# Raw-residual quarter sums for the feed-forward input, and a PSUM tile of its own for the second product's sum

## The chip, the cores and the metric

One core of a Trainium2 chip runs the whole program. The metric is the device time of one execution in microseconds, median of the runs. TensorE (PE) multiplies, VectorE (DVE) and ScalarE (ACT) do the elementwise work, GpSimd (POOL) issues the accumulating DMAs, SyncE (SP) all others.

## The reference

One step of a 1-layer encoder on 512 prompt and 32 sample tokens (544 columns here). Before the part that is changed stand attention, a recurrent branch and cross-attention; then:

```
merged = gates[:, :, 0] * ya + gates[:, :, 1] * yb + gates[:, :, 2] * yc
x = x + merged @ lp["w_out"]
h2 = rms_norm(x, lp["norm_ffn"])
g_ff, u_ff = jnp.split(h2 @ lp["w_ffn_in"], 2, axis=-1)
x = x + (jax.nn.silu(g_ff) * u_ff) @ lp["w_ffn_out"]
```

`rms_norm` multiplies each token by one factor, 1/sqrt(mean(x*x) + 1e-6), and each of the 1024 features by its gain. `w_ffn_in` is 1024 x 5632 (2816 gate and 2816 up columns), `w_ffn_out` 2816 x 1024. A final rms_norm follows.

## The kernel before

Activations lie transposed: 128 partitions x 8 feature blocks x 544 tokens. Every fp32 operand is split into a high part (`wh`, `bh`, `ah`, `hh`, made by ACT) and a low part (`wl`, `bl`, `al`, `hl`, made by DVE as the difference, `LO`), and a product takes three matmuls: hi x hi, lo x hi of the activations, hi x lo. A plain `gemm` tile of the input (8 feature blocks, two halves of 272 tokens) is 48 matmuls.

A planner, `Flow`, sets the order of all engines: generators (`take`, `get`, `yield`) are resumed by estimated times, and the instructions are recorded as they come. The hardware follows that order per engine and waits only on semaphores, which are set per tile.

The output projection (`c_o`, 8 tiles of 48 matmuls) adds to the residual `x2` in `out_evac` and gathers the squares in `sqa`; `row_norm` makes from them the factor `rb` (a few 1-column matmuls, a root of small DVE operations, a broadcast by matmuls with `ident`).

The feed-forward part has 11 pairs of input chunks (256 gate and 256 up columns), in four parts of 3, 3, 3 and 2 pairs; the order of stages is input 0 and 1, output 0, input 2, output 1, input 3, output 2, output 3. An input chunk is done in one of two ways.

- Plain (`ffn_plain`): the first pair, from `xgh`, `xgl` (the residual times the gain, made in `out_evac`); `rb` is multiplied in at the evacuation (`ff_gate`, `ff_up`). Four tiles, 192 matmuls.
- Fast (`seven`): all other 20 chunks. A chunk is a 2 x 2 block product in seven products of 12 matmuls each, 84. They are called A11, A12, A22, P1 to P4; the activations' quarter sums (forms B11, B2, U1, U2, four feature-block pairs i each) come from `ff_forms`, those of the weights from POOL's accumulating DMAs and two DVE sums. `ff_forms` waits for `rb`, then for each i multiplies two blocks of `x2` by gain and `rb`, makes sums on DVE and splits them.

Order of the products on PE: A11 of chunk c, then A22 and P4 of chunk c-1, then A12, P2, P1, P3 of chunk c. A11, P2, P3 and A22 add up in `a`, which is read between them: ACT copies it after A11 (`c11`), P2 (`c12`) and P3 (`u3`). P1 and P4 go to `b` in a side tile. A12 goes to `c_`, the second half of the acc tile whose first half is `a`; DVE adds `c_` to the copy. PSUM holds two acc tiles (two banks each) and four side tiles.

Weights come through two `raw` slots: SP loads, POOL accumulates, and `split_ffn` makes hi and lo blocks of 512, in eight places per kind, which are free again when a product is done. The gate chunk's four quarters go through Silu (`fast_gate`), the up chunk's are multiplied to them (`fast_up`) and split into the activations of the output matmuls (`acts`, in `bh`/`bl` for even parts, `ah`/`al` for odd ones).

Of the kernel before, what the change touches and what calls it, by code (L numbers as in the profile page):

```python
# [10 lines left out]
F32R = mybir.dt.float32r  # L11
# [194 lines left out]
def hybrid_step(ctx: ExitStack, tc, io):  # L206
# [26 lines left out]
    for k_, n_ in NB.items():  # L233
        fl.bufs(k_, n_)

# [142 lines left out]
    FF_PLAIN = c_fi[0][0]  # L378
    FF_FAST = {c for part in c_fi for pair in part for c in pair} - set(FF_PLAIN)

# [65 lines left out]

    def split_ffn():

        for tag, w_ in (("wh", "hb"), ("wl", "lb")):
            for _ in range(NB[tag]):  # L450
                yield from fl.take(tag)
                w = slot_tile(wpool, [P, 8, P], F32R, tag).rearrange("p a b -> p (a b)")
                add_blocks(w_, [w[:, :512], w[:, 512:]])
# [3 lines left out]
        for i in order:  # L457
            nk = chunks[i][1]
            yield from fl.get(("raw", i, 0))
            if late is not None and i not in FF_FAST:  # L460
                yield from late
                late = None
            if i not in FF_FAST:
                for j in range(2):
                    if i in FF_PLAIN:
                        r = raws[i].rearrange("p a b -> p (a b)").rearrange("p (j e i c) -> p j e i c", j=2, e=2, i=4)
                        for e in range(2):
                            yield from split((i, j, e), r[:, j, e])
                        ks = [((i, j, k % 2), k // 2) for k in range(nk)]
                    else:  # L470
                        for e in range(0, nk, 4):
                            yield from split((i, j, e), raws[i][:, e:min(e + 4, nk), j * P:(j + 1) * P])
                        ks = [((i, j, k // 4 * 4), k % 4) for k in range(nk)]
                    wts[i, j] = tuple([blocks[b][a][:, q] for b, q in ks] for a in range(2))
                    names = sorted({b for b, _ in ks})
                    frees[i, j] = names
                    fl.set(("wh", i, j), max(fl.ev["bh", b] for b in names))
                    fl.set(("wl", i, j), max(fl.ev["bl", b] for b in names))
                fl.give("raw", max(fl.ev["bl", b] for b in names))
                continue  # L480
# [25 lines left out]
    def split_weights():  # L506
        for i, (src, nk) in enumerate(chunks):
            if i == FF_PLAIN[0]:
                yield from split_ffn()
                return  # L510
# [1110 lines left out]
    mh = ml = xgh = xgl = x2 = None  # L1621
# [19 lines left out]
    def out_evac(fp, n):  # L1641
        def go(acc):
# [21 lines left out]
    def ff_forms():  # L1664

        bt, blt, ht, hlt, mt = S["bh"], S["bl"], S["xhh"], S["xhl"], S["xm"]
        half = 4 * T
        two = lambda ap: ap.rearrange("p (i t) -> p i t", i=4)
        B11 = (two(bt[:, 6 * T:]), two(blt[:, 6 * T:]))
        B2 = (two(ht[:, :half]), two(hlt[:, :half]))  # L1670
        U1 = (two(ht[:, half:]), two(hlt[:, half:]))
        U2 = (two(mt[:, :half]), two(mt[:, half:]))
# [4 lines left out]
        yield from fl.take("ft", "ft", "ft")  # L1677
        scratch = [fl.pick("ft") for _ in range(3)] + [S["sq"][1]]
        yield from fl.get("rb")
        for i in range(4):  # L1680
            y0, y1, u1, u2 = scratch
            for q, y in enumerate((y0, y1)):
                t = VX(y, x2[:, 2 * i + q], vcol("norm_ffn", 2 * i + q), S["rb"], OP.mult, OP.mult)
            yield t
            A(B11[0][:, i], y0[:, lo])
            A(B2[0][:, i], y1)
            VT(u1[:, lo], y0[:, lo], y0[:, hi], OP.subtract)
            VX(u1[:, hi], u1[:, lo], -1.0, y1[:, hi], OP.mult, OP.subtract)
            VT(u2[:, lo], y1[:, hi], y0[:, hi], OP.subtract)
            t = VX(u2[:, hi], u1[:, hi], -1.0, y1[:, lo], OP.mult, OP.subtract)  # L1690
            fl.set(("xf", "B11", i), LO(B11[1][:, i], y0[:, lo], B11[0][:, i]))
            fl.set(("xf", "B2", i), LO(B2[1][:, i], y1, B2[0][:, i]))
            yield t
            for g, ev, u in ((U1, "U1", u1), (U2, "U2", u2)):
                yield A(g[0][:, i], u)
                t = LO(g[1][:, i], u, g[0][:, i])
                fl.set(("xf", ev, i), t)
        for y in scratch[:3]:
            fl.drop("ft", y, t)

    def seven(run):
# [20 lines left out]
        for c, evac in run + [(None, None)]:  # L1722
            if c is not None:
                yield from fl.take("acc")
                acc = slot_tile(accp, [P, 2, 512], F32, "acc")
                a, c_ = acc[:, 0, :HT], acc[:, 1, :HT]
                S["b", c] = None
                fl.spawn(evac(c, a, c_))
                yield from product(a, c, "A11", True, False)
            if prev is not None:  # L1730
# [4 lines left out]
            if c is None:  # L1735
                return
# [394 lines left out]
```

## Time and profile before

| | us |
|---|---|
| median of 3 runs | 1247.83 (1246.43 to 1248.45) |
| the profiled execution | 1245.97 |
| its span in the trace | 1243.9 |
| PE busy | 1197.2 (96%) |
| DVE busy | 772.8 (62%) |
| ACT busy | 537.0 (43%) |

Line numbers are those of the kernel; most instructions come from helpers (L325 all matmuls, L252 all ACT operations, L265 and L274 DVE operations), so a place is told by the tiles' names. Idle time of an engine stands in brackets with what ended it. The granted clock is TensorE's, 1.00 for the full rate.

### The profile page before, as it was taken

Reading aid. Unit: us, or ns where it says so; the run is one execution under the profiler, and the core shown is the slowest. Engines: PE = TensorE matmul, PEld = TensorE weight load, DVE = VectorE, ACT = ScalarE, POOL = GpSimd, SP = SyncE. Lnnn points to the kernel's source line nnn. Section 1 sums busy time; section 2 is a strip of 40 time slices with the busy share of each in tenths; the row PEclk is TensorE's granted clock in tenths of the full one; section 3 lists DMA queues with packets and bytes.
Section 4 is the critical chain, followed back from the end, with each engine's and each line's share of the span. In section 5 each row is a group of like instructions: output and inputs, shape, how many; then the busy total and the mean of one; then the engine's idle time right before and its main releaser. Section 6 shows DMA issues by size and latency. Waiting matters only on the chain.

```text
span 1243.9 us, 22824 instructions
## 1 busy us (share of the span) xinstructions
PE 1197.2 (96%) x9380; PEld 1180.2 (95%) x9380; DVE 772.8 (62%) x1594; ACT 537.0 (43%) x1013; POOL 63.5 (5%) x128
## 2 busy tenths in 40 slices
PE   8999999999999999999999999995999999998996
PEld 8999999999999999999999999995998999998996
DVE  6886878776258777545354334478676647736545
ACT  6635454444254666432233223354555435524422
POOL 0002000000001101000000000010111011011001
PEclk8999999999999999999999999997999999999998
DMA  7673342322132221423331322242555546454312
GB/s 261 236 261 110 136 134 96 111 82 85 68 111 77 97 91 68 154 79 108 119 119 68 148 95 91 79 116 63 128 153 136 152 116 146 123 143 119 119 52 72
DMA packets 51817, 146.95 MB, mean 118 GB/s; under 512 B 5848, under 2 KB 17496, under 8 KB 43648
## 3 DMA queue, kind: packets, MB, share of 16 engines
q1 hardware_dynamic: 45952, 135.01, 32.5%
q0 software_dynamic: 5760, 10.49, 5.4%
q8 instruction: 73, 1.20, 0.4%
q14 instruction: 32, 0.26, 0.1%
HBM read 134.54 MB, written 13.68 MB: 119 GB/s over the span
## 4 chain that ended last, share of the span: by engine, by line
PE 91%; DVE 6%; ACT 1%; issue 1%; DMA 1%; SPq 0%; DVEq 0%; ACTq 0%
PE acc L325 76%; PE side L325 13%; PE side L332 2%; DVE wl L265 1%; DMA raw<-in_w_mem_kv 1%; DVE t L265 1%; ACT wh L252 0%; DVE al L265 0%; DVE fq L265 0%; DVE x L274 0%; DVE hl L265 0%; DVE raw L265 0%; DVE fq L274 0%; DVE rst L265 0%; DVE bl L265 0%
## 5 line engine op out<-in xcount | busy, mean ns | idle before, releaser
L252 ACT ACTIVATE wh<-raw 128x1024 fp32r<-128x1024 f32 (+2 forms) x251 | 199.2, 801 | 259.7 <-PE acc L325 194.8
L265 DVE TENSOR_TENSOR wl<-raw,wh 128x512 fp32r<-128x512 f32 (+1 forms) x252 | 225.6, 905 | 125.7 <-PE acc L325 75.9
L325 PE MATMUL acc<-hh,wh 128*128 128x272 f32 x1268 | 274.0, 292 | 10.5 <-DVE fq L265 5.4
L325 PE MATMUL acc<-hl,wh 128*128 128x272 f32 x1268 | 270.8, 290 | 0.0
L325 PEld LDWEIGHTS acc<-hh,wh 128*128 128x128 f32 x1268 | 203.0, 189 | 14.3 <-DVE fq L265 6.3
L325 PEld LDWEIGHTS acc<-hl,wh 128*128 128x128 f32 x1268 | 202.6, 188 | 0.1
L325 PE MATMUL acc<-hh,wl 128*128 128x272 f32 x1268 | 180.9, 289 | 0.0
L325 PEld LDWEIGHTS acc<-hh,wl 128*128 128x128 f32 x1268 | 166.9, 188 | 0.1
L325 PE MATMUL acc<-bh,wh 128*128 128x272 f32 x464 | 100.3, 289 | 9.7 <-ACT bh L252 9.7
L325 PE MATMUL acc<-bl,wh 128*128 128x272 f32 x464 | 100.2, 290 | 2.4 <-DVE bl L265 2.4
L325 PE MATMUL acc<-ah,wh 128*128 128x272 f32 (+2 forms) x440 | 93.0, 289 | 0.0
L325 PE MATMUL acc<-al,wh 128*128 128x272 f32 (+2 forms) x440 | 92.9, 290 | 0.0
L325 PEld LDWEIGHTS acc<-bh,wh 128*128 128x128 f32 x464 | 74.9, 189 | 10.2 <-ACT bh L252 10.2
L265 DVE TENSOR_TENSOR x<-acc,x 128x544 f32<-128x544 f32 (+2 forms) x43 | 29.4, 685 | 88.9 <-PE acc L325 88.9
L325 PEld LDWEIGHTS acc<-bl,wh 128*128 128x128 f32 x464 | 74.9, 188 | 3.0 <-DVE bl L265 3.0
L325 PEld LDWEIGHTS acc<-ah,wh 128*128 128x128 f32 x440 | 70.0, 189 | 0.0
L325 PEld LDWEIGHTS acc<-al,wh 128*128 128x128 f32 x440 | 70.0, 189 | 0.0
L325 PE MATMUL acc<-bh,wl 128*128 128x272 f32 x464 | 67.8, 290 | 0.0
L325 PE MATMUL acc<-ah,wl 128*128 128x272 f32 (+2 forms) x440 | 62.4, 291 | 0.0
L325 PEld LDWEIGHTS acc<-bh,wl 128*128 128x128 f32 x464 | 61.8, 189 | 0.0
L325 PEld LDWEIGHTS acc<-ah,wl 128*128 128x128 f32 x440 | 58.6, 192 | 0.0
L401 POOL DMA_DIRECT2D raw<-in_w_ffn_in x20 | 17.4, 872 | 599.3 <-PE side L325 318.1
(317 smaller groups left out, 2030.9 us busy)
## 6 DMA issues: line engine op xcount, KB each, us to landing
raw<-in_w_in SPq DMA_DIRECT2D x24, 1024.0 KB, 4.9
raw<-in_w_gate SPq DMA_DIRECT2D x12, 1024.0 KB, 4.9
raw<-in_w_ffn_in SPq DMA_DIRECT2D x20, 512.0 KB, 4.5
raw<-in_w_ffn_in SPq DMA_DIRECT2D x40, 256.0 KB, 4.9
raw<-in_w_ffn_out SPq DMA_DIRECT2D x12, 768.0 KB, 4.3
raw<-in_w_mem_kv SPq DMA_DIRECT2D x7, 1024.0 KB, 5.5
fb<-in_w_ffn_in SPq DMA_DIRECT2D x20, 256.0 KB, 5.0
raw<-in_w_ffn_in POOLq DMA_DIRECT2D x20, 256.0 KB, 4.3
```

The costliest lines, as they stand in the source:

```text
L252: nc.scalar.activation(out, in_, func, scale=scale, bias=bias, accum_out=accum_out)
L265: nc.vector.tensor_tensor(out, a, b, o)
L325: nc.tensor.matmul(out, lhsT=lhsT, rhs=rhs, start=start, stop=stop, skip_group_check=shared)
L332: nc.tensor.transpose(out, in_, ident[:n, :n])
L401: nc.gpsimd.dma_start(b[:, 1536:], d[:, 1536:], accum_op=OP.add)
```

## The change

All 22 input chunks take the fast way; `ffn_plain`, `ff_gate`, `ff_up` and `xgh`, `xgl` are gone. `ff_forms(i)` is spawned once per i before the projection and starts when the two residual blocks it needs are there. It leaves `rb` out: ACT multiplies by the gain alone. `rb` comes later: on the gate's quarters ahead of Silu, and for the up side not at all in parts 0 to 2. There the sum in `x2` is kept divided by `rb` (`unnormalise`, a reciprocal and eight multiplications on DVE) and multiplied by `rb` after part 2's output; in part 3 the products are multiplied by `rb` themselves.

`c_` gets a side tile. The first output tile of a stage is put between the last chunk's P3 and its A22 (`between`), output tiles are issued one by one, and `split_ffn` fills its places and splits the late weights accordingly. The places of `ah`/`al` and `bh`/`bl` are swapped. The core of the diff:

```diff
-    FF_PLAIN = c_fi[0][0]
-    FF_FAST = {c for part in c_fi for pair in part for c in pair} - set(FF_PLAIN)
+    FF_FAST = {c for part in c_fi for pair in part for c in pair}
...
     def out_evac(fp, n):
...
-            yield A(xgh[:, n], x2[:, n], scale=vcol("norm_ffn", n))
-            t = VX(xgl[:, n], x2[:, n], vcol("norm_ffn", n), f(xgh[:, n]), OP.mult, OP.subtract)
-            fl.set(("xg", n), t)
+            fl.set(("x2", n), t)
             yield from square_sum(S["sq"][0], n)
...
+    def ff_forms(i):
+
+        B11, B2, U1, U2 = S["forms"]
+        lo, hi = slice(0, HT), slice(HT, T)
+        yield from fl.get(("x2", 2 * i), ("x2", 2 * i + 1))
+        yield from fl.take("ft", "ft", "ft", "sqb")
+        y0, y1, u1 = ys = [fl.pick("ft") for _ in range(3)]
+        u2 = S["sq"][1]
+        for q, y in enumerate((y0, y1)):
+            t = A(y, x2[:, 2 * i + q], scale=vcol("norm_ffn", 2 * i + q))
+        yield t
+        A(B11[0][:, i], y0[:, lo])
+        A(B2[0][:, i], y1)
+        VT(u1[:, lo], y0[:, lo], y0[:, hi], OP.subtract)
+        VX(u1[:, hi], u1[:, lo], -1.0, y1[:, hi], OP.mult, OP.subtract)
+        VT(u2[:, lo], y1[:, hi], y0[:, hi], OP.subtract)
+        t = VX(u2[:, hi], u1[:, hi], -1.0, y1[:, lo], OP.mult, OP.subtract)
+        yield t - 800
+        t = LO(B11[1][:, i], y0[:, lo], B11[0][:, i])
...
+    def unnormalise():
+
+        yield from fl.get("rb", *[("xf", "U2", i) for i in range(4)])
+        yield from fl.take("sqb")
+        ir = S["sq"][1]
+        yield VR(ir, S["rb"])
+        for k in range(KD):
+            t = VT(x2[:, k], x2[:, k], ir, OP.mult)
+            fl.set(("x2'", k), t)
+            yield t + 2000
...
     def seven(run, between=None):
...
-                a, c_ = acc[:, 0, :HT], acc[:, 1, :HT]
+                a = acc[:, 0, :HT]
...
+            elif between is not None:
+                yield from between
             if prev is not None:
                 yield from fl.get(("u3", prev[0]))
                 yield from product(prev[1], prev[0], "A22", False, True)
...
+            yield from fl.take("side")
+            S["c", c] = c_ = side_tile()[:, :HT]
             yield from product(c_, c, "A12", True, True)
...
     def fast_gate(i, n):
...
-                A(g[:, cs], src, AF.Silu, scale=-1.0 if j else 1.0)
+                if j:
+                    yield from fl.get("rb")
+                    VT(g[:, cs], src, S["rb"][:, cs], OP.mult)
...
+            fl.set(("fg", i, n, 1), A(g[1], g[1], AF.Silu, scale=-1.0))
+            yield VT(g[0], g[0], S["rb"], OP.mult)
+            fl.set(("fg", i, n), A(g[0], g[0], AF.Silu))
...
     def fast_up(i, n):
...
+                if i == NPART - 1:
+                    t = VT(u[j], u[j], S["rb"], OP.mult)
...
     def fo_evac(fp, i, n):
...
+            if i == NPART - 2:
+                yield t
+                VT(x2[:, n], x2[:, n], S["rb"], OP.mult)
...
+        for i in range(4):
+            fl.spawn(ff_forms(i))
+        fl.spawn(unnormalise())
...
-        fl.spawn(ff_forms())
-        yield from ffn_in(0, 1)
-        yield from ffn_out(fp, 0)
-        yield from ffn_in(2)
-        yield from ffn_out(fp, 1)
-        yield from ffn_in(3)
-        yield from ffn_out(fp, 2)
-        yield from ffn_out(fp, 3)
+        acts_order = [((0, 1), 0), ((2,), 1), ((3,), 2)]
+        for parts, q in acts_order:
+            yield from ffn_in(*parts, between=ffn_out(fp, q, 0, 1) if q < 3 else None)
+            yield from ffn_out(fp, q, 1)
+        yield from ffn_out(fp, NPART - 1)
```

The instructions' order shows three places. In these rows `DVE_49`, `Activation_49` and `PE_49` are the counters of DVE, ACT and PE that an instruction waits on, `DMASW` those of POOL's DMAs.

PE from the end of A12 into P2 of a fast chunk, before:

```order
L325 MATMUL acc<-hl,wh 128x272
L325 MATMUL acc<-hh,wl 128x272 x4
L325 MATMUL acc<-hh,wh 128x272
L325 MATMUL acc<-hl,wh 128x272
L325 MATMUL acc<-hh,wh 128x272 [waits DVE_49]
L325 MATMUL acc<-hl,wh 128x272
```

The same place of the changed kernel:

```order
L327 MATMUL side<-hl,wh 128x272
L327 MATMUL side<-hh,wl 128x272 x4
L327 MATMUL acc<-hh,wh 128x272 [waits Activation_49]
L327 MATMUL acc<-hl,wh 128x272
L327 MATMUL acc<-hh,wh 128x272
```

A12 writes a side tile now, and the wait on DVE ahead of P2's third matmul is gone; P2's first one waits for ACT's copy of `a` instead.

PE behind the projection, before (plain tiles from `ah`, `al`, with the norm's matmuls among them):

```order
L325 MATMUL acc<-ah,wh 128x272 x2
L325 MATMUL acc<-al,wh 128x272 x2
L325 MATMUL side<-ones_d,sqa 128x1 [waits DVE_49]
L325 MATMUL side<-ones_d,sqa 128x1 x4
L325 MATMUL acc<-ah,wh 128x272 x2
L325 MATMUL acc<-al,wh 128x272 x2
L325 MATMUL acc<-ah,wh 128x272 [waits Activation_49]
```

The changed kernel there; `ah`, `al` hold the form B11 now, and the rows are A11 of the first chunk:

```order
L327 MATMUL acc<-ah,wh 128x272 [waits Activation_49]
L327 MATMUL acc<-al,wh 128x272
L327 MATMUL side<-ones_d,sqa 128x1 [waits DVE_49]
L327 MATMUL side<-ones_d,sqa 128x1 x4
L327 MATMUL side<-ident,rsy_9384 128x128 [waits DVE_49]
L327 MATMUL side<-ident,rsy_9384 128x128 x3
L327 MATMUL side<-ident,rsy_9384 128x32
L327 MATMUL acc<-ah,wh 128x272 [waits Activation_49]
L327 MATMUL acc<-al,wh 128x272 [waits DVE_49]
L327 MATMUL acc<-ah,wl 128x272 x4
L327 MATMUL side<-hh,wh 128x272
```

Between the norm's two groups of matmuls stood plain tiles; now nothing stands there, and A11's last form comes behind the second group.

DVE behind the root, before (`fq` and `sqb` are the forms' scratch tiles, `rb` the factor):

```order
L281 COPY rb<-side 128x32 [waits PE_49]
L265 TENSOR_TENSOR wl<-raw,wh 128x512 [waits Activation_49]
L274 SCALAR_TENSOR_TENSOR fq<-x_8133,vec,rb 128x544 [waits DVE_49,Activation_49]
L274 SCALAR_TENSOR_TENSOR fq<-x_8133,vec,rb 128x544
L265 TENSOR_TENSOR t_9433<-acc,rb 128x544
L265 TENSOR_TENSOR fq<-fq 128x272 [waits DVE_49]
L274 SCALAR_TENSOR_TENSOR fq<-fq 128x272 [waits DVE_49]
L265 TENSOR_TENSOR sqb<-fq 128x272
```

The changed kernel, some rows behind the root:

```order
L267 TENSOR_TENSOR m<-sqb,m 128x544 [waits Activation_49]
L267 TENSOR_TENSOR wl<-raw,wh 128x512 [waits PE_49,Activation_49]
L267 TENSOR_TENSOR raw<-raw 128x512 [waits DMASW2_49]
L267 TENSOR_TENSOR fq<-side,fq 128x272 [waits PE_49,Activation_49]
L288 RECIPROCAL sqb<-rb 128x544 [waits DVE_49]
L267 TENSOR_TENSOR wl<-raw,wh 128x512 [waits Activation_49]
L267 TENSOR_TENSOR wl<-raw,wh 128x512 [waits PE_49,Activation_49]
L267 TENSOR_TENSOR wl<-fb,wh 128x512 [waits DMASW3_49,PE_49,Activation_49]
L267 TENSOR_TENSOR fq<-side,fq 128x272 [waits Activation_49]
L267 TENSOR_TENSOR x_8133<-x_8133,sqb 128x544 [waits DVE_49]
```

The forms' operations have left this place; the last form's last low part (`m`) is the first row, and the reciprocal and the first multiplication of `x2` by it stand among the first two chunks' work.

## Rows read from the trace of the kernel before

**Rows 1.** The page, part 1: busy us (share of the span) xinstructions.

```profile
PE 1197.2 (96%) x9380; PEld 1180.2 (95%) x9380; DVE 772.8 (62%) x1594; ACT 537.0 (43%) x1013; POOL 63.5 (5%) x128
```

**Rows 2.** Windows: length; busy PE, PEld, DVE, ACT, POOL; granted clock, DMA share, GB/s.

```profile
814.22:859.19 44.97, 31.92 (x226) 30.56 (x225) 40.13 (x81) 22.34 (x39) 4.70 (x6) 0.83 0.43 112
859.19:1167.17 307.98, 290.52 (x2247) 283.79 (x2247) 188.18 (x330) 140.50 (x292) 30.54 (x35) 1.00 0.51 132
...
850.00:858.00 8.00, 1.88 (x4) 0.96 (x4) 7.96 (x17) 3.99 (x7) 0.00 (x0) 0.50 0.51 157
858.00:861.00 3.00, 3.00 (x14) 3.00 (x15) 2.61 (x5) 1.18 (x2) 1.74 (x2) 0.53 0.41 63
```

**Rows 3.** PE timeline, the start of the feed-forward: start, us, instruction [idle before <-releaser].

```profile
818.33 1.28 PE L325 MATMUL side<-ones_d,sqa 128*128 128x1 f32 x10 [0.93 <-DVE sqa L265]
...
850.00 0.60 PE L325 MATMUL acc<-bh,wh 128*128 128x272 f32 x1 [6.01 <-ACT bh L252]
```

**Rows 4.** DVE timeline, behind the projection and in the forms.

```profile
814.42 0.72 DVE L265 TENSOR_TENSOR x<-acc,x 128x544 f32<-128x544 f32 x1 [3.06 <-PE acc L325]
...
819.64 0.16 DVE L269 TENSOR_SCALAR rs<-side 128x5 f32<-128x5 f32 x1 [0.16 <-PE side L325]
...
821.64 0.17 DVE L274 SCALAR_TENSOR_TENSOR rsy<-rst,rsy 128x5 f32<-128x5 f32 x1
...
845.78 0.71 DVE L265 TENSOR_TENSOR bl<-t,bh 128x544 fp32r<-128x544 f32 x1
846.42 0.68 DVE L265 TENSOR_TENSOR wl<-fb,wh 128x512 fp32r<-128x512 f32 x1
847.02 0.68 DVE L265 TENSOR_TENSOR wl<-raw,wh 128x512 fp32r<-128x512 f32 x1
...
849.65 0.44 DVE L265 TENSOR_TENSOR sqb<-fq 128x272 f32<-128x272 f32 x1
850.00 0.44 DVE L274 SCALAR_TENSOR_TENSOR sqb<-fq 128x272 f32<-128x272 f32 x1
```

**Rows 5.** ACT timeline, a weight split in the same stretch.

```profile
842.57 0.61 ACT L252 ACTIVATE wh<-fb 128x512 fp32r<-128x512 f32 x1
```

**Rows 6.** PE's waits, whole kernel: for whom: us in total, times, longest.

```profile
PE acc L325 <- DVE fq L265: 6.5, 10, 1.0
PE acc L325 <- DVE t L265: 5.4, 10, 0.6
...
PE acc L325 <- ACT fq L252: 2.9, 4, 1.3
```

**Rows 7.** The chain that ended last: P2 of two neighbouring chunks; output 0.

```profile
874.20 1.52 PE acc L325 x10
...
885.51 1.52 PE acc L325 x10
...
975.52 36.23 PE acc L325 x288
```

**Rows 8.** PE timeline: weight split, start of a run, end of a run.

```profile
948.04 0.39 PE L325 MATMUL acc<-bh,ah 128*128 128x272 f32 x1 [1.00 <-ACT ah L252]
...
1014.78 0.40 PE L325 MATMUL acc<-hh,ah 128*128 128x272 f32 x1 [1.28 <-ACT fq L252]
...
1079.41 1.27 PE L325 MATMUL acc<-m,ah 128*128 128x272 f32 x8 [0.49 <-ACT t L252]
```

**Rows 9.** DVE groups by form, whole kernel: reciprocals; busy us, mean ns.

```profile
L286 DVE RECIPROCAL cc<-sm 128x1 f32<-128x1 f32 x32 | 4.9, 154 | 1.9 <-ACT e L252 1.8
...
L286 DVE RECIPROCAL r<-sm 128x8 f32<-128x8 f32 x4 | 0.8, 197 | 0.0
...
L286 DVE RECIPROCAL sp_d<-sp_d 128x8 f32<-128x8 f32 x1 | 0.2, 202 | 0.0
```

**Rows 10.** POOL timeline: first and last of seven accumulations in the first run.

```profile
877.72 0.86 POOL L401 DMA_DIRECT2D raw<-in_w_ffn_in  x1 [17.84 <-DMA raw<-in_w_ffn_in]
...
957.80 0.86 POOL L401 DMA_DIRECT2D raw<-in_w_ffn_in  x1 [12.33 <-DVE al L265]
```

More of the change, by code (lines that the diff above doesn't have):

```diff
@@ L445, in add_blocks, with to_blocks, split_plain @@
         fl.ring(tag, aps)
-    def split_ffn():
[L449 to L453, printed above, removed]
+    def to_blocks(tag, ring):
+        yield from fl.take(tag)
+        w = slot_tile(wpool, [P, 8, P], F32R, tag).rearrange("p a b -> p (a b)")
+        add_blocks(ring, [w[:, :512], w[:, 512:]])
+    def split_plain(i, j):
+        nk = chunks[i][1]
+        for e in range(0, nk, 4):
+            yield from split((i, j, e), raws[i][:, e:min(e + 4, nk), j * P:(j + 1) * P])
+        ks = [((i, j, k // 4 * 4), k % 4) for k in range(nk)]
+        wts[i, j] = tuple([blocks[b][a][:, q] for b, q in ks] for a in range(2))
+        frees[i, j] = names = sorted({b for b, _ in ks})
+        fl.set(("wh", i, j), max(fl.ev["bh", b] for b in names))
+        fl.set(("wl", i, j), max(fl.ev["bl", b] for b in names))
+    def split_ffn():
+        for _ in range(NB["wh"]):
+            fl.spawn(to_blocks("wh", "hb"))
+            fl.spawn(to_blocks("wl", "lb"))
         order = [c for kind, q in FF_ORDER for c in
@@ L457, in split_ffn @@
         for i in order:
-            nk = chunks[i][1]
             yield from fl.get(("raw", i, 0))
-            if late is not None and i not in FF_FAST:
-                yield from late
-                late = None
             if i not in FF_FAST:
                 for j in range(2):
[L465 to L479, printed above, removed]
+                    yield from split_plain(i, j)
+                    if late is not None:
+                        yield from late
+                        late = None
+                fl.give("raw", fl.ev["wl", i, 1])
                 continue
@@ L1704, in product, with seven @@
+    def unnormalise():
[7 more added lines that the diff above has]
+            yield t + 2000
+    def seven(run, between=None):
         def product(dst, c, form, first, last):
@@ L1755, in quarters @@
         yield from fl.get(("done", c, "A12"))
-        t = VT(t0[:, lo], c_, t0[:, lo], OP.add)
+        t = VT(t0[:, lo], S["c", c], t0[:, lo], OP.add)
+        fl.give("side", t)
         yield t
-        each(t0, 0, lo, t0[:, lo])
+        yield from each(t0, 0, lo, t0[:, lo])
         yield from fl.get(("done", c, "P2"))
@@ L1778, in quarters @@
         yield t
-        each(t0, 0, hi, t0[:, hi])
+        yield from each(t0, 0, hi, t0[:, hi])
         return t0, t1
@@ L1860, in ffn_in @@
             acts[i] = [S[n][:, :6 * T].rearrange("p (k t) -> p k t", k=6) for n in x]
[L1861 to L1865 removed]
+        yield from seven(run, between)
     def fo_evac(fp, i, n):
         def go(acc):
+            yield from fl.get(("x2'", n))
             t = VT(b2(x2[:, n]), acc[:, :, :HT], b2(x2[:, n]), OP.add)
```

136 lines of the change are left out of this document (45 added, 91 removed).

## The prediction

> **What bounds the kernel now.** I read the page's busy shares first, then the windows, then PE's rows in the feed-forward part, then the orders. PE is busy 96% of the span [rows 1], so only fewer matmuls or fewer PE waits can shorten it. The windows say where the waits are. From 814.22 (first matmul behind the output projection) to 859.19 PE is busy 31.92 of 44.97 us at a granted clock of 0.83; from there to 1167.17 it is busy 290.52 of 307.98 [rows 2]. What follows, the last part's output, the change leaves as it is. At full rate 288 matmuls of 128x272 take 36.23 us, 0.126 each [rows 7].
>
> Three kinds of idle time are to be seen. First, the fast products start with a stall: PE waits 6.01 us for the first quarter sum that is late [rows 3] and is busy only 1.88 of the 8 us behind that [rows 2], because ff_forms begins only when rb is there and then runs on a full DVE. Second, in each of the 20 fast chunks PE waits for a DVE add: 10 times on fq and 10 on t, 11.9 us in all [rows 6]. Place: the third matmul of P2, which writes a while DVE reads c_ in the same acc tile; the order shows that wait. Third, there are single waits where a run of chunks begins (two, of 1.28 and 1.29) or ends (three of 0.49), and one of 1.00 for weights [rows 8].
>
> **The change, part by part.** Times are counted from T = 814.22.
>
> *The plain pair goes.* Four tiles of 48 matmuls, 192, become two chunks of 84, 168. At 0.126 us that is 24.2 against 21.2.
>
> *The start.* Forms 0 to 2 are made under the projection. DVE starts an instruction 0.60 us after a 512-wide one, 0.64 after a 544-wide one and 0.35 after a 272-wide one [rows 4]. A form is five of 272 and three of 544, 3.7 us per two projection tiles (12 us), in place of two lows of 544; I cost that at nothing, since DVE sat idle 3.06 us before such an add [rows 4]. Without that cover the projection itself would slow, by up to 3 x 2.4 us. Form 3 can't start before the last add. In the changed order: DVE's add, 0.2 behind T as at 814.42, is done at 0.9. ACT stands behind two weight splits, 0.61 each [rows 5], that wait for the projection's last matmul, until 1.4, and then squares to 2.1. DVE, two weight lows later, makes the square sum, ready at 2.8. PE has meanwhile done the six matmuls of A11 for forms 0 to 2 and takes the norm's matmuls, 1.28 us [rows 3], to 4.2. DVE does four form operations to 4.4 and the root, which took from 819.64 to 821.81 [rows 4], 2.2 us, to 6.6. PE's broadcast of the root, costed like the norm's matmuls, ends at 7.8. Behind the root DVE has a weight low and a weight sum before form 3's first low part, 8.1. A11's last five matmuls follow; after the stall of this trace the granted clock was still 0.53 [rows 2], the lower of the two levels (1.2 of 2.4 GHz), where 272 columns take 0.227 us, so A11 ends at 9.4. Before, the same point, the start of A12, is T+44.97 [rows 2]. Put in two chunks at 84 x 0.126 = 10.6: 9.4 + 21.2 = 30.6. **Gain 14.4 us.** Bounds: 16.0 if the weight lows and the sum ahead of form 3 cost nothing, 10.4 if PE has to wait for all of the queue up to form 3's fourth low part, 4 us more.
>
> *The c_ tile.* With c_ in a side tile P2's third matmul has no DVE wait left. A chunk lasts 885.51 - 874.20 = 11.31 us [rows 7]; 84 matmuls are 10.56. **Gain 20 x 0.75 = 15.0.** The waits alone, 11.9 [rows 6], are the lower bound; 16.5 would count the slow refill behind each. What P2 still waits for is ACT's copy of A11, with 36 matmuls (4.5 us) between.
>
> *First chunks.* A12 in parts 2 and 3 waited for ACT's copy of a, again since both lie in one tile. Now P2 does, 12 matmuls (1.5 us) later, which covers 1.28. **Gain 2 x 1.45 = 2.9** with the refill; 0 if ACT's copy is late by that much.
>
> *Ends.* One output tile, 36 matmuls or 4.5 us, stands before A22 of the last chunk and hides the copy that was waited for. **Gain 3 x 0.65 = 2.0.**
>
> *What is added.* DVE gets two multiplications by rb of 272 and one of 544 per gate chunk. A pair of chunks then has 14 weight lows and 4 sums of 512, 10 of 272 and 4 of 544: 10.8 + 3.5 + 2.6 = 16.9 us out of 21.2, 80%. It isn't the bound, but its queue is fuller. ACT has two Silu calls for four. Once, DVE gets a reciprocal of 544 and eight multiplications of x2. No row has that reciprocal; one element costs 154 ns and eight 197 or 202 [rows 9], so 6.1 to 6.9 ns each: 154 + 543 x 6.1 = 3.5 us. Bounds: 0.7 (a plain 544-wide operation, were it no slower in bulk) and 3.9; I take 3.5, the slope of the larger group. Queued behind it are two lows of chunk 1 and the add on which P4 of chunk 0 waits. DVE reaches it at T+12.9, that add is done at 18.5, and PE comes to P4 at about 19: nothing at either bound. The Trainium skill (VectorE: DVE Perf Modes, First, the fixed hardware budget) says that Reciprocal is an iterative divide with a repeat count of 8; at eight cycles an element an estimate by that page is about 4.7 us, P4 would wait, and the sum would be 0.7 us worse; the slope of the rows, nearer to six cycles, speaks against it. The eight multiplications, 5.1 us, are spread over the first four chunks; added up in the same way DVE has about 30 us of work for the first 30 us there. I charge 1.0. The rb products in part 2's output and in part 3 lie where DVE has output tiles to spare; nothing, or 1 us without that cover. Loads: each of the two new chunks has four loads on SP, behind w_out, and two accumulations on POOL, ahead of all others there; their raw slots come free five and three projection tiles (30 and 18 us) before T; nothing.
>
> *What is late next.* In the changed order six weight lows stand directly behind an evacuation that waits for PE, 9 matmuls (1.1 us) before their use, near the end of the first run; the split waited for at 948.04 [rows 8] had 1 matmul. I charge 0.25 each, 1.5. The last two chunks of that run have their load released 109 matmuls (13.7 us) before P2 needs it; before, the tightest had 108. I charge 1.0, and take back the 1.0 of 948.04.
>
> Sum: 14.4 + 15.0 + 2.9 + 2.0 + 1.0 - 1.0 - 1.5 - 1.0 = 31.8. About 1 us of smaller gaps goes with the long ones: from 859.19 to 1167.17 there are 1668 fast and 576 output matmuls, 282.7 us, so 25.3 are lost, of which the terms name 21. **33 us.** The profiled execution took 1245.97 (span 1243.9 and 2.1 around it), 1.9 under the median of 1247.83; so the median goes to about **1215**, the profiled span to 1211.
>
> **Rivals.**
> *A new wait takes the place of the old.* PE is faster, so ACT and DVE have 0.75 us less per chunk. If A22, P3 or P4 wait 0.3 to 0.5 us in each of 22 chunks, 7 to 11 come back: 1222 to 1226. For it: 12 matmuls (1.5 us) are all that hides ACT's copies. Against: with that same cover PE waited on ACT fq only four times in the whole kernel [rows 6], two of them the 1.28 and 1.29.
> *The weights set the pace.* In the first run POOL issued seven accumulations from 877.72 to 957.80, 13.35 us apart [rows 10], while PE used a chunk in 11.31. If the pace is the loop's own (slot free, load, accumulate, split), 12 chunks in a row starve: at 13.35 by 12 x 2.8 = 33, of which the 18 to 30 us by which the first loads come early hide some 20: 1228. Against: the weight blocks, eight of each kind, are released by PE's products, so much of that pace is PE's own, waits included.
> *Slower than before.* The same loop at 13.35 in all 22 chunks with nothing loaded ahead: 22 x 2.8 = 61, 1276. It decides from 10.56 + 33/22 = 12.1 us per chunk on. Against: the runs of parts 2 and 3 begin with weights loaded under 36 us of output tiles.
> *The forms are no earlier.* In ACT's new order a weight split that waits for a DVE sum stands ahead of form 3's U1. If that makes the start as late as before, its 14.4 are lost: 1229; if by half, 1222.
>
> **How the numbers follow.** Forecast as summed, 1208 to 1220: 0.66. New waits or late forms, 1220 to 1227: 0.18. Weights set the pace in the first run, or the start fails, 1227 to 1244: 0.10. No change (within 0.2%, about what a measurement of this kernel can tell): 0.03. Slower: 0.03. The range 1208 to 1227 holds 0.84. Faster: 0.66 + 0.18 + 0.10 = 0.94.
>
> **What would show it.** Right: no PE wait on DVE fq or t of 0.5 us; a chunk in 10.6 to 10.8 us; A12 of chunk 0 some 9 to 10 us behind the projection, with PE idle for most of that; 24 matmuls fewer; a DVE reciprocal near 3.5 us. Wrong: PE waits on weight splits (wh, bh) in the second half of the first run; DVE busy over 95% there; PE waits on ACT fq or t before P3 or A22 in every chunk.

## The result and the profile after

The changed kernel takes 1217.49 us (median, 1216.03 to 1217.77) beside 1247.13 of the kernel before in the same runs (1245.54 to 1248.45): a ratio of 0.976, 95% interval 0.9744 to 0.9777, so 29.6 us less. Forecast were 1215 and a range of 1208 to 1227. The profiled span is 1215.9 us, forecast at 1211.

Page part 1 of the kernel after (busy us, share of the span, instructions), which answers [rows 1]:

```profile
PE 1190.3 (98%) x9356; PEld 1176.4 (97%) x9356; DVE 796.6 (66%) x1646; ACT 535.8 (44%) x1004; POOL 66.9 (6%) x132
```

There are 24 matmuls fewer, as forecast. PE's waits, whole kernel after (for whom: total us, times, longest), which answer [rows 6]:

```profile
PE side L327 <- DVE rsy L276: 5.5, 3, 2.8
PE side L327 <- DVE sqa L267: 3.0, 2, 1.9
PE acc L327 <- ACT wh L254: 2.8, 2, 2.6
PE acc L327 <- ACT t L254: 2.0, 2, 1.0
PE acc L327 <- ACT fq L254: 1.9, 4, 0.7
...
PE acc L327 <- DVE al L267: 0.4, 1, 0.4
```

The 20 waits on DVE's fq and t are gone. The waits on ACT's copies are as few as before, though at other places: two on t (three before), four on fq (four before). The chain of work that ended last, kernel after (start, us, what), shows undisturbed chunks, which answer [rows 7]:

```profile
897.48 4.51 PE acc L327 x36
907.99 4.51 PE acc L327 x36
918.50 4.53 PE acc L327 x36
```

They are 10.51 us apart, where two chunks before were 11.31 apart. To see where the 28.0 us of span went, I mark in both traces the first matmul behind the projection (814.22 before, 814.42 after) and the first matmul of each stage that follows an output. PE's timeline, before:

```profile
1011.58 0.29 PE L325 MATMUL acc<-bh,ah 128*128 128x272 f32 x1
...
1118.75 0.29 PE L325 MATMUL acc<-bh,wh 128*128 128x272 f32 x1
...
1203.22 0.41 PE L325 MATMUL acc<-ah,wh 128*128 128x272 f32 x2
```

and after:

```profile
993.00 0.29 PE L327 MATMUL acc<-ah,bh 128*128 128x272 f32 x1
...
1094.27 0.29 PE L327 MATMUL acc<-ah,wh 128*128 128x272 f32 x1
...
1175.25 0.41 PE L327 MATMUL acc<-bh,wh 128*128 128x272 f32 x2
```

A12 of the third chunk, where the two chunks that replace the plain pair are done, is at 848.08 after; it answers 859.19 of before, A12 of the first fast chunk. The windows after (columns as in [rows 2]):

```profile
814.42:848.08 33.66, 28.31 (x202) 27.78 (x201) 30.32 (x60) 18.57 (x34) 3.49 (x4) 0.90 0.40 104
848.08:961.31 113.23, 111.16 (x867) 108.78 (x865) 89.67 (x162) 59.91 (x120) 14.00 (x16) 1.00 0.60 153
```

| stretch | before | after | gain | by the prediction's terms |
|---|---|---|---|---|
| projection to A12 of the third chunk | 44.97 | 33.66 | 11.3 | 14.4 - 1.0 |
| to the end of output 0 | 152.39 | 144.92 | 7.5 | 7.5 + 0.65 + 1.0 - 1.5 - 1.0 = 6.7 |
| part 2 and output 1 | 107.17 | 101.27 | 5.9 | 4.5 + 1.45 + 0.65 = 6.6 |
| part 3 and output 2 | 84.47 | 80.98 | 3.5 | 3.0 + 1.45 + 0.65 = 5.1 |
| output 3 and the end | 40.68 | 40.65 | 0 | 0 |

28.2 us in all, for 32 to 33 forecast. The start is 2.1 us short (3.1 without the 1.0 that was charged there), parts 2 and 3 another 2.3; the first run gave 0.8 more than its terms.

### The profile page after: what moved, and what is told of

The parts are those of the page before. It is cut to its first block, busy times and chain, and to the rows that moved or that the text cites. A ratio compares the mean times of both kernels' runs of the same rounds, so it can differ in the third digit from the quotient of the medians.

```text
span 1215.9 us, 22828 instructions
## 1 busy us (share of the span) xinstructions
PE 1190.3 (98%) x9356; PEld 1176.4 (97%) x9356; DVE 796.6 (66%) x1646; ACT 535.8 (44%) x1004; POOL 66.9 (6%) x132
## 4 chain that ended last, share of the span: by engine, by line
PE 92%; DVE 4%; ACT 2%; issue 1%; DMA 0%; SPq 0%; DVEq 0%; ACTq 0%
PE acc L327 75%; PE side L327 16%; PE side L334 2%; DVE wl L267 1%; DVE raw L267 1%; ACT wh L254 1%; ACT bh L254 0%; DMA raw<-in_w_mem_kv 0%; DVE bl L267 0%; DVE x L276 0%; DVE rst L267 0%; DVE t L267 0%; ACT fq L254 0%; DVE al L267 0%; DVE xT L276 0%
## 5 line engine op out<-in xcount | busy, mean ns | idle before, releaser
L254 ACT ACTIVATE wh<-raw 128x512 fp32r<-128x512 f32 (+1 forms) x252 | 198.6, 799 | 269.3 <-PE acc L327 178.6
L267 DVE TENSOR_TENSOR wl<-raw,wh 128x1024 fp32r<-128x1024 f32 (+2 forms) x253 | 226.6, 904 | 110.6 <-PE acc L327 73.7
L327 PE MATMUL acc<-ah,wh 128*128 128x272 f32 x476 | 102.4, 289 | 0.0
L327 PE MATMUL acc<-al,wh 128*128 128x272 f32 x476 | 102.2, 289 | 0.0
L327 PE MATMUL acc<-bh,wh 128*128 128x272 f32 (+2 forms) x364 | 76.8, 288 | 0.0
L327 PE MATMUL acc<-bl,wh 128*128 128x272 f32 (+2 forms) x364 | 76.7, 288 | 0.0
L327 PE MATMUL acc<-ah,wl 128*128 128x272 f32 x476 | 67.5, 289 | 0.0
L327 PE MATMUL acc<-bh,wl 128*128 128x272 f32 (+2 forms) x364 | 53.0, 290 | 0.0
L327 PE MATMUL side<-hh,wh 128*128 128x272 f32 x200 | 52.8, 291 | 0.1
L327 PE MATMUL side<-hl,wh 128*128 128x272 f32 x200 | 52.7, 291 | 0.0
```

Of the source, the lines that this page charges most:

```text
L254: nc.scalar.activation(out, in_, func, scale=scale, bias=bias, accum_out=accum_out)
L267: nc.vector.tensor_tensor(out, a, b, o)
L327: nc.tensor.matmul(out, lhsT=lhsT, rhs=rhs, start=start, stop=stop, skip_group_check=shared)
```

## The experiments

The program ahead of the projection is the same in all these kernels, yet the projection ends at 813.1 to 814.5 us of the trace from one execution to the next (in one trace, of e10_no_rb_on_gate, at 817.7, behind a start that waited longer). Beside each median I therefore give the **stretch** from the projection's end to the end of the span: 429.7 before, 401.5 in the changed kernel. The kernel before took 1246.0 to 1246.1 beside the experiments.

One thing varies inside the stretch too. In every trace with the changed kernel's start A12 of the first chunk begins 10.2 to 10.3 us behind the projection, at the lower granted clock, but the clock comes back sooner or later. A12 took 2.67 us in the changed kernel's trace and 1.85, 1.95, 1.63, 2.33 and 2.15 in those of e3_no_between, e4_no_unnormalise, e7_unnormalise_late, e8_split_behind_sum and e10_no_rb_on_gate. So a stretch can differ by up to 1 us before the experiment's edit has any effect; where that matters, the account below goes by stages.

**c_ back in the acc tile (e1_c_in_acc).**

```diff
-            S["c", c] = c_ = side_tile()[:, :HT]
+            S["c", c] = c_ = acc[:, 1, :HT]
```

> The changed kernel with one part undone: A12's sum c_ lies again in the second half of the acc tile. Theory (the term of the sum as the prediction put it): 0.75 us for each chunk, now 22 of them, 16.5, and 2.9 for the first chunks of parts 2 and 3, so 1217.5 + 16.5 to 19.4 = 1234 to 1237; PE waits on DVE fq and t come back, 11 of each, 0.5 to 0.6 each, ahead of P2. Rival (the term is only the waits themselves, and PE's faster pace came from other parts too): 22 x 0.6 = 13 or less, 1230 or less.

1238.0 us (ratio 0.9929, 0.9913 to 0.9946), 20.5 more than the changed kernel; stretch 423.4, 21.9 more. Its waits:

```profile
PE acc L327 <- DVE fq L267: 8.9, 11, 2.2
PE acc L327 <- DVE t L267: 7.5, 11, 1.1
```

All 22 are back, 17 of them of 0.53 to 0.62 us as in the kernel before, and its undisturbed chunks are 11.32 us apart. 22 x 0.81 = 17.8; the rest, 4.1, is more than the theory's 2.9. By stages (as in the table) the loss is 4.1, 5.5, 5.9 and 6.4 us, where 0.81 for each chunk would be 1.6, 8.1, 4.9 and 3.2. The five longer waits, 0.96 to 2.2 us, stand in parts 2 and 3. PE also ran longer at the lower clock, at the start until 832.4 (19.0 us behind the projection, against 12.8 in the changed kernel's trace) and again in part 3 (granted clock, third number from the end, 0.50 and 0.66):

```profile
822.00:832.00 10.00, 8.91 (x38) 8.27 (x38) 8.31 (x11) 3.38 (x7) 1.74 (x2) 0.50 0.50 144
1139.00:1144.00 5.00, 4.96 (x27) 4.96 (x28) 3.26 (x5) 2.24 (x5) 0.00 (x0) 0.66 0.49 161
```

The second stands right behind the wait of 2.2 us. So c_ was worth what the term said for each chunk; the 1 to 2.5 us beyond the theory's 19.4 are in part the clock.

**c_ in a side tile, alone, in the kernel before (e2_only_c_side).**

```diff
-                a, c_ = acc[:, 0, :HT], acc[:, 1, :HT]
+                a = acc[:, 0, :HT]
...
+            yield from fl.take("side")
+            S["c", c] = c_ = side_tile()[:, :HT]
             yield from product(c_, c, "A12", True, True)
...
-        t = VT(t0[:, lo], c_, t0[:, lo], OP.add)
+        t = VT(t0[:, lo], S["c", c], t0[:, lo], OP.add)
```

> The kernel before with one part of the change alone: c_ in a side tile. Theory: 20 x 0.75 + 2.9 = 17.9 off 1247.1, 1229, with no PE wait on DVE fq or t. Rival (the wait is only replaced: ACT's copies or the weights are next, 0.3 us a chunk): 1235 to 1239. If this gain and the loss of e1_c_in_acc agree within 2 us, the part stands by itself, whatever the other parts do.

1230.56 us (0.987, 0.9855 to 0.9885): 15.5 off, stretch 14.1 off. No wait on DVE fq or t is left, and six neighbouring chunks in its first run lie 10.5 us apart, but ACT's copies are waited for by 0.44 and 0.93 in each of parts 2 and 3. The theory held to within 2 to 4 us. The two runs differ by 5 us, more than the 2 I had set, so the parts don't simply add up: the tile is worth 14 to 15.5 for 20 chunks alone and 20.5 to 22 for 22 chunks in the changed kernel.

**No output tile between P3 and A22 of a run's last chunk (e3_no_between).**

```diff
-            yield from ffn_in(*parts, between=ffn_out(fp, q, 0, 1) if q < 3 else None)
-            yield from ffn_out(fp, q, 1)
+            yield from ffn_in(*parts)
+            yield from ffn_out(fp, q)
```

> The changed kernel without an output tile between the last chunk's P3 and its A22. Theory: 3 x 0.65 = 2.0 more, 1219.5, and PE waits for ACT's copy (t) of about 0.5 at three places. Rival (the copy is no longer late there, since ACT's queue has changed): within 0.5 of 1217.5.

1219.43 us (0.9778, 0.9764 to 0.9793), 1.9 more; stretch 2.1 more. PE waits for the copy again at three places, of 1.27, 0.49 and 0.49; the first on PE's timeline:

```profile
953.79 1.27 PE L327 MATMUL acc<-m,bh 128*128 128x272 f32 x8 [1.27 <-ACT t L254]
```

By stages the three ends lost 1.5, 0.6 and 0.8 us, 2.9 in all; the stretch shows less because A12 of the first chunk was 0.8 faster in this trace. So the tile between is worth what the term of 2.0 said or somewhat more: the waits come back, and the first is longer than the 0.49 of the kernel before.

**The forms wait for rb (e5_forms_after_rb).**

```diff
-        yield from fl.get(("x2", 2 * i), ("x2", 2 * i + 1))
+        yield from fl.get("rb", ("x2", 2 * i), ("x2", 2 * i + 1))
```

> The changed kernel with one part undone: the forms wait for rb again, as before, though they do not use it. Behind rb (some 8 us behind the projection) four forms take 4 x 3.7 us of DVE, with weight work of the first chunks among them. Theory (early forms carry the gain of the start): A12 of chunk 0 comes 12 to 18 us later than its 10.2 behind the projection, and the time is 1229 to 1236. Rival (the gain of the start comes from the plain pair that is gone; the forms would be ready in time since DVE has no plain tile's work any more): 4 us or less, 1222 or less.

1231.05 us (0.9876, 0.9845 to 0.9906), 13.6 more; stretch 416.7, 15.2 more. A12 of the first chunk begins 25.8 us behind the projection, 15.6 later than in the changed kernel. The start's gain is the early forms': without them A12 of the third chunk comes 49.8 us behind the projection, later than the 44.97 of the plain pair. Part of that is the clock: it was granted at 0.50 until 843.9, some 30 us behind the projection.

**The reciprocal and the eight multiplications of x2 left out (e4_no_unnormalise).**

```diff
-        yield VR(ir, S["rb"])
+        yield fl.charge("V", 70 + 8 * T, ir, (S["rb"],))
...
-            t = VT(x2[:, k], x2[:, k], ir, OP.mult)
+            t = fl.charge("V", vcost(ir), x2[:, k], (x2[:, k], ir), True)
```

> The changed kernel with the reciprocal of rb and the eight multiplications of the residual by it left out (so the feed-forward's output is added to a residual that was not divided); the planner still counts their time, so that all other instructions keep their order. Theory (PE's waits of 1.01 at 841.98 and 864.27 come from a DVE queue that is crowded by these nine instructions, 8.6 us: a weight sum comes late, ACT's weight split waits for it, and ACT's copy waits behind that): both fall under 0.3, and the time falls by 1.5 to 2.5 us, to 1215 to 1216. Rival (ACT's order alone makes these waits): they stay, and the time with them, within 0.5 of 1217.5.

1215.93 us (0.9754, 0.974 to 0.9769), 1.6 off by the median, but the stretch, 400.9, is only 0.6 shorter: the rest lies ahead of the projection's end. And the 0.6 is not the nine instructions' either. It is there when A12 of the first chunk ends, ahead of the place of the reciprocal. First matmul of A12 and of P2 in the changed kernel, 2.67 us apart:

```profile
824.62 0.43 PE L327 MATMUL side<-hh,wh 128*128 128x272 f32 x1
...
827.29 0.29 PE L327 MATMUL acc<-hh,wh 128*128 128x272 f32 x1
```

and here, 1.95 apart:

```profile
823.31 0.43 PE L327 MATMUL side<-hh,wh 128*128 128x272 f32 x1
...
825.26 0.29 PE L327 MATMUL acc<-hh,wh 128*128 128x272 f32 x1
```

Behind that no stage is faster. The two waits did not move. PE's timeline:

```profile
839.95 1.27 PE L327 MATMUL acc<-m,wh 128*128 128x272 f32 x8 [1.01 <-ACT t L254]
```

So the theory of a crowded DVE falls for them. The changed kernel's own trace shows what holds the copy. PE, ACT and DVE there:

```profile
841.98 1.27 PE L327 MATMUL acc<-m,wh 128*128 128x272 f32 x8 [1.01 <-ACT t L254]
```

```profile
841.01 0.63 ACT L254 ACTIVATE wh<-raw 128x512 fp32r<-128x512 f32 x1 [1.45 <-PE side L327]
841.54 0.38 ACT L254 ACTIVATE t<-acc 128x272 f32<-128x272 f32 x1
```

```profile
838.01 0.44 DVE L267 TENSOR_TENSOR t<-side,t 128x272 f32<-128x272 f32 x1
838.37 0.68 DVE L267 TENSOR_TENSOR wl<-raw,wh 128x512 fp32r<-128x512 f32 x1
838.97 0.72 DVE L267 TENSOR_TENSOR fq<-fq,rb 128x544 f32<-128x544 f32 x1
839.60 0.69 DVE L267 TENSOR_TENSOR wl<-raw,wh 128x512 fp32r<-128x512 f32 x1
840.21 0.69 DVE L267 TENSOR_TENSOR raw<-raw 128x512 f32<-128x512 f32 x1
```

P2 ended at 839.3, so `a` could be copied then. But ACT's next instruction is a weight split of the sum `raw`, and that sum ends at 840.9, at the end of a row of DVE work that begins with the add of c_, which cannot start before A12 ends. ACT idles 1.45 us, splits, and copies `t` at 841.54. (The trace names PE as the releaser of the split; the split began 0.1 us behind the end of the DVE sum, and so it did in the kernel without the nine instructions.) The Trainium skill (PSUM — Partial Sum Buffer, Engine vs sequencer instructions) calls the queues of ScalarE and VectorE strict FIFO; the trace agrees, with a copy that started 2.2 us after its input was ready, most of that behind a split it had nothing to do with.

**Two of the gate's products by rb left out (e10_no_rb_on_gate).**

```diff
                 if j:
-                    VT(g[:, cs], src, S["rb"][:, cs], OP.mult)
+                    if src is a:
+                        VT(g[:, cs], src, S["rb"][:, cs], OP.mult)
+                    else:
+                        fl.charge("V", vcost(src), src, (src, S["rb"]), True)
...
-            yield VT(g[0], g[0], S["rb"], OP.mult)
+            yield fl.charge("V", vcost(g[0]), g[0], (g[0], S["rb"]), True)
```

> The changed kernel with two of the three multiplications by rb on the gate's quarters left out (272 of the negative half and the 544 of the other half; the planner still counts their time), so the gate's input is not normalised there: 11 x (0.35 + 0.64) = 10.9 us of DVE less. Theory (as the prediction had it, DVE is not the bound and its added work costs nothing outside part 3): the PE waits of part 3 at 1123.00 and 1126.93 may go (1.3 us), all others stay; 1216 to 1217.5. Rival (the fuller DVE queue is what keeps the changed kernel 2.5 us above the forecast): 2 to 4 us off, 1213.5 to 1215.5.

1214.73 us (0.9756, 0.9739 to 0.9773), 2.8 off; stretch 399.5, 2.0 off. The median says rival, the stretch lies between, and 0.5 of it is A12 of the first chunk; 1.5 is left for the products. The same wait as above:

```profile
844.12 1.15 PE L327 MATMUL acc<-m,wh 128*128 128x272 f32 x7 [0.38 <-ACT t L254]
```

1.01 has become 0.38, and its twin at 864.27 likewise: the difference, 0.63, is the 544-wide product that stood ahead of `raw` in DVE's row. The two together are most of the 1.5. The waits of part 3 stayed (0.68 and 0.65); there the products of the up side, which this kernel keeps, stand ahead of a weight sum in DVE's row. So the products by rb were not free; where one stands ahead of a weight sum, PE pays for it.

**The reciprocal later, beside part 1's first chunk (e7_unnormalise_late).**

```diff
-        yield from fl.get("rb", *[("xf", "U2", i) for i in range(4)])
+        yield from fl.get("rb", ("c22", c_fi[1][0][0]))
```

> The changed kernel with the reciprocal and the eight multiplications of the residual begun only in part 1's first chunk, where DVE has idle time, instead of among the first chunks. e4_no_unnormalise left the waits at 841.98 and 864.27 as they were and took 0.6 us off the stretch behind the projection; so theory (those nine instructions cost the start about that much): 0.3 to 0.8 off, 1216.7 to 1217.2, and the two waits of 1.01 stay. Rival (the 1.0 that the prediction charged for crowding was right): 1.0 to 2.0 off.

1221.06 us (0.9799, 0.9773 to 0.9826), 3.6 more; stretch 4.4 more. Neither theory had a loss. DVE, ACT and PE there:

```profile
899.37 3.54 DVE L288 RECIPROCAL sqb<-rb 128x544 f32<-128x544 f32 x1
...
907.11 0.68 DVE L267 TENSOR_TENSOR raw<-raw 128x512 f32<-128x512 f32 x1
```

```profile
907.90 0.63 ACT L254 ACTIVATE wh<-raw 128x512 fp32r<-128x512 f32 x1 [6.69 <-DVE raw L267]
```

```profile
909.41 1.95 PE L327 MATMUL acc<-m,bh 128*128 128x272 f32 x7 [3.65 <-ACT t L254]
```

The chain is the same: the reciprocal pushes a weight sum back, ACT's queue stands 6.69 us at its split, PE waits 3.65 for the copy behind it. Behind the wait the granted clock fell, to 0.57 over this window, so the seven matmuls of 909.41 took 1.95 us; that is a part of the loss:

```profile
909.00:913.00 4.00, 3.59 (x17) 3.59 (x18) 3.31 (x6) 2.46 (x6) 0.00 (x0) 0.57 0.64 183
```

Of the two waits of 1.01 that both theories kept, the first became 1.35 and the second went; the order on DVE is another one here. DVE had idle time on average; the place had not.

**Splits queued when their sum is due (e8_split_behind_sum).**

```diff
-            VT(p2, p1, q[0], OP.add)
+            yield VT(p2, p1, q[0], OP.add)
...
-        VT(a12, p2, a12, OP.add)
+        yield VT(a12, p2, a12, OP.add)
```

> The changed kernel with one change in the planner's split of the weights: the split of a DVE sum (P2's and P4's weights) is put into ACT's queue only when that sum is due, no longer at once. Theory (ACT's copies of a, for which PE waits 1.01, 1.01, 0.25, 0.32, 0.67, 0.69 and 0.65, stand behind such a split that waits for its DVE sum; it is a matter of the written order): most of these 4.6 us go, and the time falls by 2 to 4 us, to 1213.5 to 1215.5. Rival (the splits come later in turn, and PE waits for weights, wh or bh, instead): no gain, 1217 or more.

1212.25 us (0.9726, 0.9701 to 0.9752), 5.2 off; stretch 396.6, 4.9 off. The waits on ACT's t are gone, and of those on ACT's fq one is left:

```profile
PE acc L327 <- ACT fq L254: 0.5, 1, 0.5
```

That shows the cause: the written order of ACT's queue. The rival is there too, but smaller: six chunks at the end of the first run lie 11.3 us apart, where the changed kernel had three, with PE waits of 0.22 to 0.30 for a weight split or low part that comes late.

**Clock kept up (e6_clock_kept).** Twenty matmuls whose result nobody reads, in the two gaps of the norm.

```diff
+        if ev == "rb":
+            yield from busy(9)
         for a, sq in enumerate(sqs):
...
+        if ev == "rb":
+            yield from busy(11)
         y = rsqrt_(v, pool)
```

> The changed kernel with 20 added matmuls of 128x128 ones whose result nobody reads: 9 ahead of the norm's first matmuls and 11 ahead of the broadcast of the root, where PE is idle for 1.93 and 2.41 us and the granted clock then is 0.50 until about 827. Theory (the start's step missed 0.8 us because the broadcast and the first products ran at the lower clock): the clock stays at 1.00, the broadcast takes 1.1 instead of 2.15, A11's last six and A12's first matmuls 0.126 each instead of 0.227; A12 starts 1.5 us earlier and the whole gain is 2 to 3 us, 1214.5 to 1215.5. Rival (the next product waits for form 3's low parts on DVE, which are only just ready): 1 us or less, and a PE wait on DVE takes the place.

1215.97 us (0.9757, 0.9732 to 0.9783), 1.5 off; stretch 1.2 off. Two windows of the changed kernel (granted clock is the third number from the end), then one of this one:

```profile
820.00:827.00 7.00, 6.04 (x27) 6.04 (x28) 6.80 (x16) 2.75 (x5) 0.00 (x0) 0.53 0.21 50
827.00:830.00 3.00, 3.00 (x25) 3.00 (x24) 2.44 (x2) 1.55 (x3) 0.00 (x0) 0.96 0.88 317
```

```profile
821.00:823.00 2.00, 1.95 (x15) 1.76 (x15) 2.00 (x5) 2.00 (x4) 0.00 (x0) 1.00 0.00 0
```

The clock stays at 1.00, the broadcast takes 1.13 us instead of 2.15, A12 of the first chunk starts 1.4 us earlier and P1 2.5 earlier, as the theory had it. Against the other traces of that start the 2.5 would be 1.5 to 2.1. But half of it is lost again by P3 of the second chunk, 0.66 of that at the copy that stands behind the split:

```profile
839.49 1.27 PE L327 MATMUL acc<-m,wh 128*128 128x272 f32 x8 [1.67 <-ACT t L254]
```

**Both of these (e9_clock_and_split).**

> e6_clock_kept and e8_split_behind_sum together: the added matmuls in the norm's gaps, and weight splits queued on ACT only when their DVE sum is due. e6_clock_kept alone gained 1.5 where its theory wanted 2 to 3; in its trace the copy at 839.49 is waited for by 1.67 instead of 1.01, the mechanism that e8_split_behind_sum removes. Theory (the clock is worth 2 to 3 us once no copy stands behind a split): 1212.3 - 2 to 3 = 1209.3 to 1210.3, below both kernels. Rival (form 3 or the weights of the first chunks are next): 1211 to 1212.3.

1210.36 us (0.9715, 0.9702 to 0.9728), at the edge of the theory; stretch 395.4, 1.2 below that of the split alone, which is the rival's side. At P1 of the first chunk it was 2.2 ahead; waits of 0.16 for a DVE add (832.14) and 0.20 for an ACT copy (838.62), with the refill behind them, take most of the difference: at the third chunk it is 1.3 ahead. So the clock is worth some 2 us at the place and 1.2 in the end (1.9 by the medians).

**Low parts earlier in DVE's queue, on top of both (e11_low_earlier).**

```diff
         fl.set(("bh", name), t)
-        yield t
+        yield t - (400 if "rb" in fl.ev else 0)
```

> e9_clock_and_split with weight lows queued on DVE 0.4 us of planner time earlier from rb on. In e8_split_behind_sum PE still waits 0.22 to 0.30 some fourteen times in the first run for a weight split or low that stands behind a DVE evacuation of a product that PE has just ended. Theory (order again): half or more of these 3.5 us go, 1.5 to 3 below e9_clock_and_split. Rival (DVE then stands at a low that waits for ACT, and its sums come later): no gain or a loss of 1 to 3.

1206.57 us (0.9682, 0.9669 to 0.9695), 3.8 below; stretch 391.9, 3.5 below. Page part 1:

```profile
PE 1188.4 (99%) x9396; PEld 1177.1 (98%) x9396; DVE 795.2 (66%) x1644; ACT 537.9 (45%) x1006; POOL 67.0 (6%) x132
```

Of twelve waits of 0.2 to 0.3 us in the first run before, four are left; most of them were order. This version is 10.9 us faster than the changed kernel, and nothing in it does less arithmetic.

## Why the prediction was right, and where its terms were off

**The mechanism was right.** The waits on DVE's c_ add went, chunks that nothing disturbs take 10.51 us (forecast 10.56), the early forms carry the start (13.6 to 15.2 us when undone), and the ends, forecast at 2.0, were worth 1.9 by the median and 2.9 by stages.

**The start: 14.4 forecast, 11.3 measured.** PE's timeline after, which answers [rows 3]:

```profile
817.27 1.27 PE L327 MATMUL side<-ones_d,sqa 128*128 128x1 f32 x10 [1.93 <-DVE sqa L267]
820.96 2.34 PE L327 MATMUL side<-ident,rsy 128*128 128x128 f32 x10 [2.41 <-DVE rsy L276]
...
824.62 0.43 PE L327 MATMUL side<-hh,wh 128*128 128x272 f32 x1
```

The norm's matmuls were forecast to end at 4.2 us and do so at 4.1; the root was forecast to be there at 6.6 and the broadcast starts at 6.5. The step that failed is "PE's broadcast of the root, costed like the norm's matmuls", 1.2 us: it took 2.15, since the granted clock had fallen to its lower level in the two gaps. That makes A12 start at 10.2 instead of 9.4. I had put the lower clock on A11's last matmuls (six, not the five that the prediction counts) but not on A12's: its twelve took 2.67 us instead of 1.5. The third piece is the copy behind a split at 841.98, a wait of 1.01 us and 1.17 with the refill. 0.8 + 1.2 + 1.2 make up the difference. The 0.8 is in every trace of this start; how much of A12's 1.2 comes differs from one to the next, down to 0.1.

**The first rival came in part.** "A new wait takes the place of the old" was priced at 0.3 to 0.5 us in each of 22 chunks. It came at six places instead, of 0.25 to 1.01 us, and by a mechanism I had written only into the fourth rival, for form 3: an ACT weight split that waits for a DVE sum stands ahead of something PE needs. The two at 841.98 and 864.27 can be read in the written order of ACT's queue. Without it the kernel is 4.9 to 5.2 us faster; with that, the forecast of 1211 for the span would have been met (1211.1).

**DVE's added work: 1.0 charged for the reciprocal's crowding, nothing for the products by rb.** The first measured nothing, for the 0.6 by which that kernel's stretch was shorter lies ahead of the reciprocal; the second 1.5 by stages, 2.8 by the medians. "It isn't the bound, but its queue is fuller" stopped a step short: the question was what stands behind each product in DVE's row. In part 3 I had covered the products by idle time under output tiles; PE waits there of 0.69 and 0.65 stand in the trace, and the stage gained 3.5 of 5.1. The up side's products, 0.64 to DVE's next start, stand ahead of the weight sums on which the splits there wait:

```profile
1119.45 0.72 DVE L267 TENSOR_TENSOR t<-t,rb 128x544 f32<-128x544 f32 x1
1120.09 0.69 DVE L267 TENSOR_TENSOR wl<-raw,wh 128x512 fp32r<-128x512 f32 x1
1120.69 0.69 DVE L267 TENSOR_TENSOR raw<-raw 128x512 f32<-128x512 f32 x1
```

By the pattern of part 0 they would be most of these waits; no run left them out. e8_split_behind_sum took the waits away with the order alone, the products kept.

**The reciprocal: 3.5 us forecast from the slope of small ones [rows 9].** DVE's timeline after:

```profile
827.92 3.54 DVE L288 RECIPROCAL sqb<-rb 128x544 f32<-128x544 f32 x1
```

3.54 us is 154 ns and 6.2 ns for each further element. The Trainium skill (VectorE: DVE Perf Modes, First, the fixed hardware budget) gives Reciprocal a repeat count of 8, which made an estimate of 4.7 us; the measurement decides for the slope of the rows. That it would cost nothing where it stood held (the kernel without it is no faster behind the first chunk's A12), and the experiment with the late reciprocal shows that this was the place's merit and not the instruction's.

**The late rows: -1.5 charged for six weight lows, -1.0 for two late loads.** PE stops six times, for 0.2 to 0.3 us each, 1.6 in all: at 924.14, 927.55, 938.87 and 950.17 for a low part, but at 934.39 and 945.70 for a weight split behind a DVE sum, which the prediction had among its signs of being wrong. (Another sign, DVE busy over 95% there, did not come: 55.5 of the 70 us from 880 to 950.) The loads cost nothing visible; no PE wait of the first run's end stands behind a load. The wait of 948.04 was gone, as forecast.

**The weights did not set the pace, but they were slower than PE.** No PE wait in the first run stands behind a load, and its waits for splits are the two of 0.22. POOL's accumulations after, third to last of the twelve chunks of that run, which answer [rows 10]:

```profile
830.45 0.85 POOL L402 DMA_DIRECT2D raw<-in_w_ffn_in  x1 [24.15 <-DMA raw<-in_w_ffn_in]
...
881.31 0.86 POOL L402 DMA_DIRECT2D raw<-in_w_ffn_in  x1 [9.11 <-DMA raw<-in_w_ffn_in]
...
892.50 0.86 POOL L402 DMA_DIRECT2D raw<-in_w_ffn_in  x1 [8.79 <-DVE t L276]
...
941.02 0.86 POOL L402 DMA_DIRECT2D raw<-in_w_ffn_in  x1 [9.27 <-DVE wl L267]
```

They come 10.9 to 14.2 us apart, 12.3 in the mean, instead of 13.35, while PE used a chunk in 11.0 in the mean. What hid that is the lead: the third chunk's accumulation stands 19 us before its P2 (849.60), the last one's 8 (948.88). The loop became faster when PE did, which fits the argument against that rival, but it stayed slower than PE; how fast it would be by itself no run shows.

**The parts were not independent.** The prediction added its terms. The tile of c_ alone gave 14 to 15.5, and undone 20.5 to 22. Two more chunks are 1.6 of that; five of the 22 waits were longer than before, by 0.4 to 1.7 us, and the lower clock lasted longer at the start and came back in part 3. That the longer waits come from DVE's added products is not shown; no run has c_ in the acc tile without them.

**Where luck helped.** The charges of 1.0 for crowding and 1.0 for late loads stand for things that no trace shows; they covered 2 us of what the start and parts 2 and 3 fell short. Without them the same sum would have given 1213, 4.5 us from the median instead of 2.5, still inside the range.

## What to carry to other kernels

Where queues are served in written order, look at each instruction that the critical engine waits for and ask what stands ahead of it in its own queue, and what that waits for in turn; the busy share of the engine does not answer that. A planner that queues an instruction before its input is due turns a late sum on one engine into a late copy on another; here a few characters that delay the queueing were worth 5 us and another order of low parts 3.5 more. Undo a part from the new kernel as well as adding it to the old one: the two differed by 5 us here.

## What the runs showed of the hardware

The granted clock stood at 0.50 from the second of two idle times of PE, 1.93 and 2.41 us, which were parted by 1.27 us of one-column matmuls; in the changed kernel's trace it was still there when PE had been busy again from 820.96 to about 827. In six traces with this start it came back at different times, so that the twelve matmuls of A12 took 1.63 to 2.67 us. 20 unread matmuls in those gaps kept it at 1.00. It also fell behind single waits of PE of 3.65 us (e7_unnormalise_late) and 2.2 us (e1_c_in_acc). A reciprocal of 544 fp32 elements a partition takes 3.54 us where a product of the same size takes 0.72.
